# Tokens of a mixture of experts moved through DRAM rows instead of one-hot matmuls

## The chip, the cores and the metric

One core of a Trainium2 chip runs the whole program in one launch. The metric is device time in microseconds (us). Lower is better. Engines: PE (TensorE), DVE (VectorE), ACT (ScalarE), POOL (GpSimd) and SP (SyncE, which here only issues DMAs). DMAs issued by SP and by POOL stand in two different queues.

## The reference

Two layers over 256 tokens of width 1024, all in float32: a gated delta rule with a dense feed-forward, then windowed attention with a mixture of experts. Only the last part changes:

```python
def moe_swiglu(x, w_router, w_gate, w_up, w_down):          # x: 256 x 1024, 8 experts of width 3584
    logits = xf @ w_router
    top_val, top_idx = lax.top_k(logits, 2)
    gates = einsum('nk,nke->ne', softmax(top_val), one_hot(top_idx, 8))
    for e in range(8):
        h = jax.nn.silu(xf @ w_gate[e]) * (xf @ w_up[e])
        out = out + gates[:, e:e + 1] * (h @ w_down[e])
    return out
```

The sum `ALPHA * x + out` then goes through a layer norm, which is the output.

## The kernel before

Only the tokens routed to an expert are multiplied with its weights, up to 128 of them (a loop behind a branch, not taken here, handles more). The router (`logits`, `route`, `gates`) leaves three small tables with 8 columns per token: `sel` (is this expert chosen), `pos` (the token's place among that expert's tokens) and `gate`. `x[0]` and `x[1]` are the two blocks of 128 tokens, in SBUF.

**Expert loop.** `todo` runs over 8 experts `e` and 7 blocks `b` of 512 hidden columns, 56 blocks. In each, `gateup` multiplies the expert's gathered tokens `xg` with 512 columns of `w_gate` and of `w_up`; `hidden_moe` forms silu(gate) * up (`msg`: the activation at L1099, the product at L1101) and transposes it (L1105) into a high and a low part (`mhh`, `mhl`); `down` adds its product with 512 rows of `w_down` into two PSUM banks `acc[e]`. `down` of a block is issued after `gateup` of the next one.

**Weights.** Every weight arrives by `unit` in loads of 1 MiB, issued by SP (L127) into a ring of buffers `raw`, and is split into a rounded part `hi` (ACT, L136) and a remainder `lo` (DVE, L137), four pieces each. A product is three matmuls (`mm3`, L152 to L155). A block takes 6 loads, 24 pieces of `hi` and of `lo`, and 72 matmuls of 512 columns. `more_ring` widens the ring for the experts: after the first round it cycles over 10 buffers.

**Going to an expert.** `gather(e)`, issued after block 2 of the expert before: DVE builds two 128x128 one-hot matrices `Pe` (L1047), 16 float32 matmuls (L1053) multiply them with `x`, and the result is split into `xg` (L1067, L1068).

**Coming back.** `finish(e)`, issued after the last `down`: `Pe` is transposed (L1134) and copied (L1135), `acc` is split (`yh`, `yl`: L1140, L1141), 8 matmuls (L1144, L1145) spread the rows over the 256 tokens, and DVE adds them, scaled by `gate`, to `y` (L1147), four times 512 columns. `y` is set to `ALPHA * x` by POOL at expert 0, block 3 (L1167).

**Layer 0.** The change also adds DMAs there. The gated delta rule inverts triangular matrices. Diagonal blocks go to DRAM and back (`dA`, then `A`: L501, L506), DVE solves them in 15 steps (L517, L518), and the result goes through DRAM again (`dD`, then `DD`: L520, L522) to PE (L595). POOL masks `EdT` just before (L485).

**Order.** A scheduler places each engine's instructions; every engine runs its own list strictly in that order, so one that waits holds up all behind it.

Of the kernel before, what the change touches and what calls it, by code (L numbers as in the profile page):

```python
# [30 lines left out]
P = 128  # L31
# [17 lines left out]
C_ID, C_TRIU, C_TRIS, C_IOTA, C_J, C_MB, C_OH, C_W = 0, 128, 256, 384, 512, 640, 768, 896  # L49


def constants():
    import numpy as np
    c = np.zeros((P, C_W), np.float32)
# [17 lines left out]
def kernel(ctx: ExitStack, tc: tile.TileContext, A, out):  # L72
# [38 lines left out]
    def more_ring(c, name, bufs, before=(), after=(), keep=()):  # L111
        pool = c.enter_context(tc.tile_pool(name=name, bufs=bufs))
        more = [raw_in(pool, "raw")] * bufs
        raws[0] = chain(base, before, more, keep, after, cycle(base + more + list(keep)))
# [264 lines left out]
    nc.sync.dma_start(cst, A["consts"][:, P:])  # L379
# [59 lines left out]
    # projections, causal convolution and silu, channel-major  # L439
# [36 lines left out]
    # A' = strict lower of p_i k_i.k_j exp(gc_i - gc_j); inverse of I + A', first in diagonal blocks of 16  # L476
    Up = gp.tile([P, 2, 8, P], F32, name="Up")
    dA = dram.tile([16 * HS], F32, name="dA")
    for tb in range(2):
# [5 lines left out]
        G.affine_select(EdT[:, tb], EdT[:, tb], [[0, 8], [1, P]], OP.is_ge, 0.0, base=0, channel_multiplier=-1)  # L485
# [92 lines left out]
    # inverse of the diagonal blocks of 32, 64 and 128 from those of half the size  # L578
# [41 lines left out]

    before = None
# [11 lines left out]
    # chunk 0, state, chunk 1  # L633
# [332 lines left out]
    # router: the rank of each expert for a token, and its slot among the tokens of that expert  # L966
# [6 lines left out]
    sel, gate, pos = (rt.tile([P, 2, E], F32, name=n) for n in ("sel", "gate", "pos"))  # L973
# [12 lines left out]
    def route(tb, plg, done):  # L986
# [47 lines left out]

    with ExitStack() as mctx:
        more_ring(mctx, "ring_m", 4, [], [raw_in(per, "Bh"), raw_in(per, "lngb")],
                  [raw_in(per, t) for t in ("Al", "Bl", "Ah")])
        mp = mctx.enter_context(tc.tile_pool(name="moe", bufs=2))
        Pe = {}

        def gather(e):
            Pe[e] = mp.tile([P, 2, P], F32, name="Pe", tag="Pe")
# [7 lines left out]
            pg = [accb() if e == 0 else None for _ in range(2)]  # L1050

            def pick(k, tb):
                PE.matmul(pg[k // 4][:, (k % 4) * P:(k % 4 + 1) * P], x[tb][:, k * P:(k + 1) * P], Pe[e][:, tb, :],  # L1053
                          start=tb == 0 and (e > 0 or k % 4 == 0), stop=tb == 1 and (e > 0 or k % 4 == 3))

            if e == 0:
                for k in range(KC):
                    pick(k, 0)
            for g in range(2):
                if e:  # L1060
                    pg[g] = trb()
                for k in range(4 * g, 4 * g + 4):
                    if e:
                        pick(k, 0)
                    pick(k, 1)
                hi, lo = (t[:, 4 * g:4 * g + 4, :].rearrange("p a c -> p (a c)") for t in xg)
                S.copy(hi, pg[g])  # L1067
                V.tensor_sub(lo, pg[g], hi.bitcast(F32))  # L1068
            return xg, placed

        xg = {}
        xg[0], placed = gather(0)
# [4 lines left out]
        V.tensor_copy(cnti, cnt[0:1, :])  # L1077
        for tb in range(2):
            with tc.issue_after(placed.ins):
                gates(tb, lgs[tb])  # L1080
# [48 lines left out]

        def finish(e):  # L1130
# [140 lines left out]
```

## Time and profile before

| | |
|---|---|
| three runs | 1487.53, 1488.69, 1488.91 us; median 1488.69 |
| profiled execution, span from first to last instruction | 1484.7 us (the profile gives no other time of it) |
| median of the runs less that span | 4.0 us |
| PE, DVE, ACT, POOL busy | 97%, 85%, 68%, 2% of the span |
| DMA | 427.67 MB, 288 GB/s over the span |

A row of a timeline gives the start, the time from the first start to the last end of the merged instructions, engine, line, operation, tiles written and read, and their count. A row with windows gives a stretch, its length, the busy time of each engine with the count of instructions, TensorE's granted clock as a share of full speed, the DMA engines' share, and GB/s. In `--lines` style rows: count, total busy time and mean ns of one, then the idle time before and what ended it.

### The profile page before, as it was taken

To read this page: it belongs to the slowest core of one execution; us is meant where nothing else is said; L and a number is where in the kernel's file an instruction comes from. 1 tells how busy PE (TensorE), PEld (TensorE's weight loads), DVE (VectorE), ACT (ScalarE), POOL (GpSimd) and SP (SyncE) were. 2 spreads that over 40 slices of the span, in tenths; PEclk is the share of its full clock that TensorE was granted. 3 is DMA by queue.
4 is the path that set the end of the run, shared out by engine and by line. 5 is a ranking of instruction groups with operands and counts; after the bars stand their busy time and mean duration, and the time that the engine had idled before them with its cause. 6 is when DMAs were issued, how large, how long until landed. Compare 5 with 4: busy or idle time off the path is not lost. (4 is left out here: it accounts for less than half of the span.)

```text
span 1484.7 us, 20295 instructions
## 1 busy us (share of the span) xinstructions
PE 1447.1 (97%) x7023; PEld 1193.3 (80%) x7023; DVE 1256.1 (85%) x2296; ACT 1016.6 (68%) x1998; POOL 32.6 (2%) x56
## 2 busy tenths in 40 slices
PE   6999999999998999999999999999999999999995
PEld 5888788887877888888888878878888887887884
DVE  4875965555867999999998998999999999899997
ACT  4764454443534878878877777877887787777883
POOL 4000000001000200000000000000000000000000
PEclk9999999999998999999999999999999999999998
DMA  8631575553638899999999989999999999999980
GB/s 266 208 118 58 186 257 181 173 196 85 233 114 298 317 358 371 342 348 378 329 361 342 350 327 354 375 328 357 366 338 350 372 376 335 352 368 335 380 310 30
DMA packets 189308, 427.67 MB, mean 288 GB/s; under 512 B 12096, under 2 KB 19424, under 8 KB 189200
## 3 DMA queue, kind: packets, MB, share of 16 engines
q1 hardware_dynamic: 186512, 421.69, 79.0%
q0 software_dynamic: 1216, 3.98, 1.0%
q8 instruction: 57, 0.93, 0.3%
q10 hardware_dynamic: 1472, 0.66, 0.2%
q14 instruction: 51, 0.42, 0.1%
HBM read 422.99 MB, written 3.30 MB: 287 GB/s over the span
## 5 line engine op out<-in xcount | busy, mean ns | idle before, releaser
L137 DVE TENSOR_TENSOR lo<-raw,hi 128x512 fp32r<-128x512 f32 x1576 | 977.4, 684 | 104.3 <-ACT hi L136 95.6
L136 ACT CAST hi<-raw 128x512 fp32r<-128x512 f32 x1576 | 851.8, 619 | 167.4 <-PE acc L153 57.3
L152 PE MATMUL mm<-hi,xg 128*128 128x512 f32 x448 | 175.7, 392 | 0.2
L152 PE MATMUL acc<-hi,mhh 128*128 128x512 f32 x448 | 175.8, 402 | 0.0
L153 PE MATMUL acc<-hi,mhl 128*128 128x512 f32 x448 | 175.0, 391 | 0.0
L153 PE MATMUL mm<-hi,xg 128*128 128x512 f32 x448 | 175.0, 391 | 0.0
L152 PE MATMUL acc<-hi,xg 128*128 128x512 f32 x448 | 174.4, 389 | 0.0
L153 PE MATMUL acc<-hi,xg 128*128 128x512 f32 x448 | 174.3, 389 | 0.0
L155 PE MATMUL acc<-lo,mhh 128*128 128x512 f32 x448 | 148.1, 390 | 0.0
L155 PE MATMUL mm<-lo,xg 128*128 128x512 f32 x448 | 124.8, 391 | 0.5 <-DVE lo L137 0.3
L155 PE MATMUL acc<-lo,xg 128*128 128x512 f32 x448 | 121.9, 391 | 0.7
L155 PEld LDWEIGHTS acc<-lo,xg 128*128 128x128 f32 x448 | 84.1, 188 | 20.8 <-DVE lo L137 3.3
L155 PEld LDWEIGHTS mm<-lo,xg 128*128 128x128 f32 x448 | 84.1, 188 | 20.0 <-DVE lo L137 2.7
L152 PEld LDWEIGHTS mm<-hi,xg 128*128 128x128 f32 x448 | 84.1, 188 | 18.7 <-ACT hi L136 2.1
L155 PEld LDWEIGHTS acc<-lo,mhh 128*128 128x128 f32 x448 | 84.1, 188 | 18.5
L153 PEld LDWEIGHTS acc<-hi,xg 128*128 128x128 f32 x448 | 84.1, 188 | 17.4
L152 PEld LDWEIGHTS acc<-hi,xg 128*128 128x128 f32 x448 | 84.1, 188 | 17.3
L153 PEld LDWEIGHTS mm<-hi,xg 128*128 128x128 f32 x448 | 84.2, 188 | 17.2 <-DVE xg L1068 0.3
L153 PEld LDWEIGHTS acc<-hi,mhl 128*128 128x128 f32 x448 | 84.3, 188 | 15.9
L152 PEld LDWEIGHTS acc<-hi,mhh 128*128 128x128 f32 x448 | 84.2, 188 | 16.0
L1108 ACT CAST mhh<-tr 128x512 fp32r<-128x512 f32 x56 | 32.8, 585 | 90.5 <-PE tr L1105 90.5
L1099 ACT ACTIVATE msg<-mm 128x512 f32<-128x512 f32 x56 | 33.4, 596 | 46.5 <-PE mm L155 46.5
(359 smaller groups left out, 1717.9 us busy)
## 6 DMA issues: line engine op xcount, KB each, us to landing
raw<-in_moe_w_gate_dram SPq DMA_DIRECT2D x112, 1024.0 KB, 6.6
raw<-in_moe_w_up_dram SPq DMA_DIRECT2D x112, 1024.0 KB, 6.7
raw<-in_moe_w_down_dram SPq DMA_DIRECT2D x112, 1024.0 KB, 6.0
raw<-in_a_w_in_dram SPq DMA_DIRECT2D x12, 1024.0 KB, 5.4
raw<-in_ffn_w_gate_dram SPq DMA_DIRECT2D x11, 1024.0 KB, 5.2
raw<-in_ffn_w_up_dram SPq DMA_DIRECT2D x11, 1024.0 KB, 5.4
raw<-in_ffn_w_down_dram SPq DMA_DIRECT2D x11, 1024.0 KB, 4.9
raw<-in_b_w_in_dram SPq DMA_DIRECT2D x5, 1024.0 KB, 5.2
```

What stands on the lines that cost most here:

```text
L136: S.copy(hi[:, c], raw[:, c])
L137: subs.append(V.tensor_sub(lo[:, c], raw[:, c], hi[:, c].bitcast(F32)))
L152: PE.matmul(ps, xh(k), wh, start=first and k == 0, stop=False)
L153: PE.matmul(ps, xl(k), wh, start=False, stop=False)
L155: PE.matmul(ps, xh(k), wl, start=False, stop=last and k == n - 1)
L1099: S.activation(s, ps[0], AF.Silu)
L1108: S.copy(hh, p)
```

## The change

A token's rows now pass through DRAM for experts 1 to 7 on the way in and for experts 0 to 6 on the way out. Expert 0 still gathers with one-hot matmuls and expert 7 still comes back with them.

- **Layer 0**: ten POOL DMAs of 512 KB write zeros from a constant in DRAM to two DRAM tables, `xs` (seven) and `ys` (three), issued after the mask of `EdT` (`turn_z`). A table has 128 rows per expert and 256 spare rows.
- **Start of the experts**: `places` computes on POOL and DVE, for each token's first and second expert, the row in the tables (`keyi`) and the gate (`gat2`). Four indirect DMAs on POOL's queue scatter the rows of `x` to `xs`; two DMAs save `x` in `x3d`.
- **In**: `fetch(e)` loads 128 rows of `xs` (512 KB) at block 1 of the expert before; `gather(e)` at block 3 is 8 transposes on PE, and the split as before.
- **Out**: `keep(e)` copies `acc` with two ACT copies and stores 512 KB to `ys`. At expert 7 four indirect DMAs (`collect`) bring back each token's two rows, and DVE adds each with one 128x1024 operation (`yt * gat2 + y`). Expert 7's rows in `ys` are zero; `finish(7)` adds its part.
- **Ring**: 12 buffers instead of 10, until expert 6, block 4, where two go back to `y` and the layer norm's parameters; `y` is loaded there from `x3d` and scaled on POOL. The buffers of `x` serve as `xr` and `yt`.

```diff
+    with tc.issue_after(turn_z.ins):
+        for r in range(P, SPARE, P):
+            nc.gpsimd.dma_start(xs[r:r + P], zero)
+        for r in range(SPARE - P, ROWS, P):
+            nc.gpsimd.dma_start(ys_[r:r + P], zero)
...
+    def places():
+        sq = [P, 2, E]
+        row, spill, one, val = (rt.tile(sq, F32, name=n) for n in ("row", "spill", "one", "val"))
+        G.tensor_tensor(row, pos, cs(C_EX, E)[:, None, :].to_broadcast(sq), op=OP.add)
+        G.tensor_tensor(spill, cs(C_SP, 2)[:, :, None].to_broadcast(sq), row, op=OP.subtract)
+        G.tensor_scalar(val, pos, float(P), None, op0=OP.is_ge)
+        G.tensor_tensor(spill, spill, val, op=OP.mult)
+        G.tensor_tensor(row, row, spill, op=OP.add)
+        key = rt.tile([P, 2, 2], F32, name="key")
+        for j in range(2):
+            G.tensor_scalar(one, rank, float(j), None, op0=OP.is_equal)
+            for src, dst in ((row, key), (gate, gat2)):
+                G.tensor_tensor(val, one, src, op=OP.mult)
+                V.tensor_reduce(dst[:, j], val, axis=AX.X, op=OP.add)
+        V.tensor_copy(keyi, key)
...
+        def fetch(e):
+            xr[e] = per.tile([P, D], F32, name="xr", tag="x0")
+            nc.gpsimd.dma_start(xr[e], xs[e * P:(e + 1) * P])
...
-                    pg[g] = trb()
-                for k in range(4 * g, 4 * g + 4):
                     if e:
-                        pick(k, 0)
-                    pick(k, 1)
+                        PE.transpose(pc, xr[e][:, k * P:(k + 1) * P], ident)
...
+        for j in range(2):
+            for tb in range(2):
+                nc.gpsimd.indirect_dma_start(out=xs[:, :], out_offset=at(j, tb), in_=x[tb][:, :], in_offset=None)
         for tb in range(2):
+            nc.gpsimd.dma_start(x3d[tb * P:(tb + 1) * P], x[tb])
...
+        def keep(e):
+            yt = per.tile([P, D], F32, name="yt", tag="x1")
+            for h in range(2):
+                S.copy(yt[:, h * 512:(h + 1) * 512], acc[e][h])
+            nc.gpsimd.dma_start(ys_[e * P:(e + 1) * P], yt)
...
+        def collect(j, tb):
+            yt = per.tile([P, D], F32, name="yt", tag="x%d" % tb)
+            nc.gpsimd.indirect_dma_start(out=yt[:, :], out_offset=None, in_=ys_[:, :], in_offset=at(j, tb))
+            V.scalar_tensor_tensor(y[tb], yt, gat2[:, j, tb:tb + 1], y[tb], op0=OP.mult, op1=OP.add)
...
                 if prev[1] == NB - 1:
-                    finish(prev[0])
-            if b == 2 and e + 1 < NE:
-                xg[e + 1] = gather(e + 1)[0]
+                    keep(prev[0])
+            if b == 1 and e + 1 < NE:
+                fetch(e + 1)
+            if b == 3 and e + 1 < NE:
+                xg[e + 1] = gather(e + 1)
...
+            if e == NE - 1 and 1 <= b <= 4:
+                collect((b - 1) // 2, (b - 1) % 2)
```

**How the order moves.** First, DVE's list at the start of the experts, around the split of expert 0's `xg`, which PE's first products need (`mx`, `gate` and `gden` belong to the router's gates, `lo` to the weights). Before:

```order
L1011 TENSOR_REDUCE mx_4217<-lg_4148 128x1
L1011 TENSOR_REDUCE mx_4226<-lg_4162 128x1
L137 TENSOR_TENSOR lo<-raw,hi 128x512
L1013 TENSOR_SCALAR gate<-lg_4148,mx_4217 128x8
L1013 TENSOR_SCALAR gate<-lg_4162,mx_4226 128x8
L137 TENSOR_TENSOR lo<-raw,hi 128x512
L1015 TENSOR_TENSOR gate<-gate,sel 128x8 x2
L137 TENSOR_TENSOR lo<-raw,hi 128x512
L1068 TENSOR_TENSOR xg<-acc,xg 128x512
L1076 TENSOR_REDUCE cnt<-tr 128x1
L1068 TENSOR_TENSOR xg<-acc,xg 128x512
```

And now, the same stretch and the rows that follow it:

```order
L148 TENSOR_TENSOR lo<-raw,hi 128x512
L1033 TENSOR_SCALAR gate<-lg_4161,mx_4231 128x8
L1033 TENSOR_SCALAR gate<-lg_4174,mx_4240 128x8
L1073 TENSOR_REDUCE key<-val 128x2
L148 TENSOR_TENSOR lo<-raw,hi 128x512
L1035 TENSOR_TENSOR gate<-gate,sel 128x8 x2
L148 TENSOR_TENSOR lo<-raw,hi 128x512
L1114 TENSOR_TENSOR xg<-acc,xg 128x512
```

```order
L148 TENSOR_TENSOR lo<-raw,hi 128x512
L1073 TENSOR_REDUCE gat_4191<-val 128x2
L148 TENSOR_TENSOR lo<-raw,hi 128x512
L1073 TENSOR_REDUCE key<-val 128x2
L148 TENSOR_TENSOR lo<-raw,hi 128x512
L1073 TENSOR_REDUCE gat_4191<-val 128x2
L1074 CAST keyi<-key 128x4
```

A reduction of `key` that waits for POOL stands ahead of the split of `xg`, and three more with a cast among the next pieces of `lo`; between two of them POOL has to multiply again, since `val` is one buffer.

Second, POOL's list from the mask of `EdT` in layer 0 to the start of layer 1. Before, and now:

```order
L485 AFFINE_SELECT EdT<-EdT 128x1024 x2
L739 DMA relb<-in_rel_bias_dram 32x16
L743 MEMSET rr 16x384
L746 DMA rd<-rr 16x384
L785 DMA rw<-in_moe_router_dram 128x8x8
```

```order
L496 AFFINE_SELECT EdT<-EdT 128x1024 x2
L638 DMA xs<-in_consts_dram 128x1024 x7
L640 DMA ys<-in_consts_dram 128x1024 x3
L760 DMA relb<-in_rel_bias_dram 32x16
L764 MEMSET rr 16x384
L767 DMA rd<-rr 16x384
L806 DMA rw<-in_moe_router_dram 128x8x8
```

The ten fills of zeros come right behind the mask, on a queue that had nothing to do for a while.

Third, DVE's list where expert 6 ends and expert 7 begins (`mhl` of expert 7's block 0 is the first row but one of each). Before, and now:

```order
L137 TENSOR_TENSOR lo<-raw,hi 128x512 x4
L1109 TENSOR_TENSOR mhl<-tr,mhh 128x512
L1141 TENSOR_TENSOR yl<-acc,yh 128x512
L137 TENSOR_TENSOR lo<-raw,hi 128x512 x3
L1147 SCALAR_TENSOR_TENSOR y<-tr,gate,y 128x512 x2
L1141 TENSOR_TENSOR yl<-acc,yh 128x512
L137 TENSOR_TENSOR lo<-raw,hi 128x512
L1147 SCALAR_TENSOR_TENSOR y<-tr,gate,y 128x512 x2
L137 TENSOR_TENSOR lo<-raw,hi 128x512 x16
L1101 TENSOR_TENSOR msg<-msg,acc 128x512
```

```order
L148 TENSOR_TENSOR lo<-raw,hi 128x512 x4
L1162 TENSOR_TENSOR mhl<-tr,mhh 128x512
L148 TENSOR_TENSOR lo<-raw,hi 128x512 x12
L1211 SCALAR_TENSOR_TENSOR y<-yt,gat_4191,y 128x1024
L148 TENSOR_TENSOR lo<-raw,hi 128x512 x4
L1211 SCALAR_TENSOR_TENSOR y<-yt,gat_4191,y 128x1024
L148 TENSOR_TENSOR lo<-raw,hi 128x512 x4
L1154 TENSOR_TENSOR msg<-msg,acc 128x512
L148 TENSOR_TENSOR lo<-raw,hi 128x512 x4
L1162 TENSOR_TENSOR mhl<-tr,mhh 128x512
L148 TENSOR_TENSOR lo<-raw,hi 128x512 x4
L1211 SCALAR_TENSOR_TENSOR y<-yt,gat_4191,y 128x1024
L148 TENSOR_TENSOR lo<-raw,hi 128x512 x8
L1211 SCALAR_TENSOR_TENSOR y<-yt,gat_4191,y 128x1024
```

The splits and sums of `finish(6)` are gone. In their place four sums of 128x1024 that wait for the indirect loads stand among the pieces of `lo`; 12 pieces separate `mhl` from the first. All other rows of these engines in the experts stand as before but for the missing `Pe`, `yl` and `y` rows and `xg`, which comes one block later.

## Rows read from the trace of the kernel before

**Rows 1.** The first rows of the page, and busy us of the engines, their share of the span and their instructions.

```profile
span 1484.7 us, 20295 instructions
...
PE 1447.1 (97%) x7023; PEld 1193.3 (80%) x7023; DVE 1256.1 (85%) x2296; ACT 1016.6 (68%) x1998; POOL 32.6 (2%) x56
```

**Rows 2.** Timeline of ACT, the activation of `msg` (L1099), one in each of the 56 blocks: expert 0 block 1, expert 1 blocks 4 and 5, expert 7 blocks 0 and 2, and the last.

```profile
493.39 0.59 ACT L1099 ACTIVATE msg<-mm 128x512 f32<-128x512 f32 x1
...
670.85 0.59 ACT L1099 ACTIVATE msg<-mm 128x512 f32<-128x512 f32 x1
...
687.64 0.59 ACT L1099 ACTIVATE msg<-mm 128x512 f32<-128x512 f32 x1
...
1344.75 0.60 ACT L1099 ACTIVATE msg<-mm 128x512 f32<-128x512 f32 x1 [1.36 <-PE mm L155]
...
1381.79 0.60 ACT L1099 ACTIVATE msg<-mm 128x512 f32<-128x512 f32 x1 [1.37 <-PE mm L155]
...
1449.00 0.60 ACT L1099 ACTIVATE msg<-mm 128x512 f32<-128x512 f32 x1 [1.38 <-PE mm L155]
```

**Rows 3.** Timeline of PE: the gather of expert 1 and the row after it; the first and the eighth product of a weight buffer in expert 1, block 6 (the first of `w_up`); the transposes of `msg` in the last block and the row after them.

```profile
521.22 3.73 PE L1053 MATMUL tr<-Pe,x 128*128 128x128 f32 x32
524.71 0.48 PE L152 MATMUL mm<-hi,xg 128*128 128x512 f32 x1
...
704.12 0.39 PE L152 MATMUL acc<-hi,xg 128*128 128x512 f32 x1
...
705.70 0.39 PE L153 MATMUL acc<-hi,xg 128*128 128x512 f32 x1
...
1456.96 0.60 PE L1105 MATMUL tr<-ident,msg 128*128 128x128 f32 x4
1457.32 0.48 PE L152 MATMUL acc<-hi,mhh 128*128 128x512 f32 x1
```

**Rows 4.** Timeline of DVE in the same block.

```profile
704.37 2.51 DVE L137 TENSOR_TENSOR lo<-raw,hi 128x512 fp32r<-128x512 f32 x4 [0.22 <-issue]
```

**Rows 5.** Who waited for whom in SP's queue: us in total, times, longest us; the timeline of SP, the first and the last of the 14 loads of expert weights issued before 470 us (the first row holds two); and four windows.

```profile
SPq L127 <- DVE lo L137: 1081.4, 370, 28.0
...
405.05 4.14 SPq L127 DMA_DIRECT2D raw<-in_moe_w_gate_dram  x2
...
469.99 0.50 SPq L127 DMA_DIRECT2D raw<-in_moe_w_up_dram  x1
...
445.00:450.00 5.00, 5.00 (x34) 4.46 (x34) 3.19 (x10) 3.54 (x10) 0.00 (x0) 1.00 1.05 399
560.00:600.00 40.00, 40.00 (x182) 33.12 (x181) 38.29 (x63) 33.88 (x64) 0.00 (x0) 1.00 1.02 374
1240.00:1340.00 100.00, 100.00 (x470) 83.37 (x469) 93.29 (x156) 79.56 (x152) 0.00 (x0) 1.00 1.00 363
1440.00:1445.00 5.00, 5.00 (x26) 4.12 (x25) 4.83 (x9) 4.21 (x9) 0.00 (x0) 1.00 0.38 145
```

**Rows 6.** Groups of instructions by line, shapes apart: the sums of `finish`, and a DVE operation on 128x1024 of layer 0.

```profile
L1147 DVE SCALAR_TENSOR_TENSOR y<-tr,gate,y 128x512 f32<-128x512 f32 x32 | 22.5, 745 | 2.0 <-PE tr L1145 1.7
...
L563 DVE TENSOR_TENSOR EdT<-acc,EdT 128x1024 f32<-128x1024 f32 x2 | 2.4, 1218 | 0.2 <-PE acc L560 0.2
```

**Rows 7.** DMA issues: destination and source, queue, count, KB each, median us from issue to landing.

```profile
raw<-in_moe_w_gate_dram SPq DMA_DIRECT2D x112, 1024.0 KB, 6.6
raw<-in_moe_w_up_dram SPq DMA_DIRECT2D x112, 1024.0 KB, 6.7
raw<-in_moe_w_down_dram SPq DMA_DIRECT2D x112, 1024.0 KB, 6.0
...
lngb<-in_ln_g_dram SPq DMA_DIRECT2D x4, 512.0 KB, 5.8
...
dD<-DD POOLq DMA_DIRECT2D x2, 512.0 KB, 8.3
dA<-Ed SPq DMA_DIRECT2D x2, 512.0 KB, 2.9
```

**Rows 8.** Timeline of DVE at the start of the experts, and of POOL in layer 0, operations on 128x16: the first pair spaced widely, the second closely.

```profile
472.25 0.17 DVE L1006 COPY pos<-mm 128x8 f32<-128x8 f32 x1 [1.38 <-PE mm L1005]
...
473.45 0.36 DVE L1013 TENSOR_SCALAR gate<-lg,mx 128x8 f32<-128x8 f32 x2
...
20.11 0.61 POOL L391 TENSOR_SCALAR m<-t 128x16 f32<-128x16 f32 x1
20.80 0.55 POOL L392 TENSOR_SCALAR y<-m 128x16 f32<-128x16 f32 x1
...
26.13 0.22 POOL L403 TENSOR_TENSOR w<-w,s 128x16 f32<-128x16 f32 x1
26.44 0.25 POOL L404 TENSOR_SCALAR w<-w 128x16 f32<-128x16 f32 x1
```

**Rows 9.** Layer 0: timeline of POOL (the second mask of `EdT`) and of DVE (first step of the solution), and a window.

```profile
50.77 1.09 POOL L485 TENSOR_SCALAR_AFFINE_SELECT EdT<-EdT 128x1024 f32<-128x1024 f32 x1 [1.52 <-ACT EdT L484]
...
69.73 0.17 DVE L517 TENSOR_TENSOR tm<-A,D 128x15 f32<-128x15 f32 x1
...
65.00:70.00 5.00, 5.00 (x24) 3.87 (x22) 5.00 (x16) 3.49 (x9) 0.00 (x0) 1.00 0.79 227
```

**Rows 10.** Timeline of DVE, the last split of a weight.

```profile
1462.43 2.50 DVE L137 TENSOR_TENSOR lo<-raw,hi 128x512 fp32r<-128x512 f32 x4 [1.12 <-ACT hi L136]
```

More of the change, by code (lines that the diff above doesn't have):

```diff
@@ L109, with more_ring, go @@
     raws = [cycle(base)]
-    def more_ring(c, name, bufs, before=(), after=(), keep=()):
+    def more_ring(c, name, bufs, keep=()):
         pool = c.enter_context(tc.tile_pool(name=name, bufs=bufs))
-        more = [raw_in(pool, "raw")] * bufs
-        raws[0] = chain(base, before, more, keep, after, cycle(base + more + list(keep)))
+        turns = base + [raw_in(pool, "raw")] * bufs + list(keep)
+        def go():
+            while True:
+                turns.append(turns.pop(0))
+                yield turns[-1]
+        raws[0] = go()
+        return turns
     quanta = [4]
@@ L972 @@
     G.affine_select(before, before, [[1, E], [-1, E]], OP.is_gt, 0.0, base=0, channel_multiplier=0)
-    sel, gate, pos = (rt.tile([P, 2, E], F32, name=n) for n in ("sel", "gate", "pos"))
+    sel, gate, pos, rank = (rt.tile([P, 2, E], F32, name=n) for n in ("sel", "gate", "pos", "rank"))
     def logits(tb):
@@ L1033, with at, onehot @@
     cnti = rt.tile([1, 1], I32, name="cnti")
+    keyi = rt.tile([P, 2, 2], I32, name="keyi")
+    gat2 = rt.tile([P, 2, 2], F32, name="gat2")
+    x3d = dram.tile([T, D], F32, name="x3d")
+    def places():
[13 more added lines that the diff above has]
+        V.tensor_copy(keyi, key)
+    def at(j, tb):
+        return bass.IndirectOffsetOnAxis(ap=keyi[:, j, tb:tb + 1], axis=0)
     with ExitStack() as mctx:
-        more_ring(mctx, "ring_m", 4, [], [raw_in(per, "Bh"), raw_in(per, "lngb")],
-                  [raw_in(per, t) for t in ("Al", "Bl", "Ah")])
+        ylng = [raw_in(per, t) for t in ("Bh", "lngb")]
+        turns = more_ring(mctx, "ring_m", 4, [raw_in(per, t) for t in ("Al", "Bl", "Ah")] + ylng)
         mp = mctx.enter_context(tc.tile_pool(name="moe", bufs=2))
         Pe = {}
-        def gather(e):
-            Pe[e] = mp.tile([P, 2, P], F32, name="Pe", tag="Pe")
+        xr = {}
+        def onehot(e):
+            Pe[e] = mp.tile([P, 2, P], F32, name="Pe", tag="Pe", bufs=1)
             with ExitStack() as late:
@@ L1077 @@
         V.tensor_copy(cnti, cnt[0:1, :])
+        with tc.issue_after(placed.ins):
+            for tb in range(2):
+                gates(tb, lgs[tb])
+            places()
+        for j in range(2):
+            for tb in range(2):
+                nc.gpsimd.indirect_dma_start(out=xs[:, :], out_offset=at(j, tb), in_=x[tb][:, :], in_offset=None)
         for tb in range(2):
-            with tc.issue_after(placed.ins):
-                gates(tb, lgs[tb])
+            nc.gpsimd.dma_start(x3d[tb * P:(tb + 1) * P], x[tb])
         NB = EF // 512
@@ L1184 @@
                                 op0=OP.is_equal, op1=OP.mult)
+            xo = [op_.tile([P, D], F32, name="xo%d" % tb) for tb in range(2)]
+            for tb in range(2):
+                nc.sync.dma_start(xo[tb], x3d[tb * P:(tb + 1) * P])
             xg2 = op_.tile([P, KC, P], F32, name="xg2")
```

60 lines of the change are left out of this document (36 added, 24 removed).

## The prediction

> **What bounds the kernel now.** I read the page first: PE is busy for 97% of the span, DVE 85%, ACT 68%, and 20295 instructions take 1484.7 us [rows 1]. A share is an average over stages, so next comes the step of the expert loop: the activations of `msg`, one per block. Two neighbouring plain blocks are 687.64 − 670.85 = 16.79 us apart [rows 2]. PE explains that alone: eight products of one weight buffer start 705.70 − 704.12 = 1.58 us apart, 0.226 each; 72 of them are 16.3, and the four transposes of `msg` 1457.32 − 1456.96 = 0.36 [rows 3]. DVE needs less: its splits run at (2.51 − 0.68) / 3 = 0.61 apiece, if the first row's latency at one end (0.68) is left out [rows 4]; 24 splits and two more operations of that size make 15.9, so it gains 0.9 us per block on PE. The loads are ahead as well: SP waits 370 times for the split that frees a buffer, 1081.4 us in all [rows 5]. So **PE sets the pace**, and a PE instruction taken away there is time gained.
>
> **How much is not plain blocks.** From expert 0's block 1 to the last block are 54 steps, 1449.00 − 493.39 = 955.61 us [rows 2]. At 16.79 they would take 906.7; 48.9 us are over. Nothing else stands there but seven gathers and seven `finish`. A gather takes PE 524.71 − 521.22 = 3.49 [rows 3], seven 24.4. What is left, 24.5, is 3.5 for a `finish`. A check: from 1344.75 to 1381.79, across one `finish`, are 37.04 us, two plain steps and 3.46 [rows 2].
>
> **The change part by part.**
> - *In, gathers 1 to 7.* 16 float32 matmuls go, 8 transposes come. At 0.09 each [rows 3] they take 0.72, say 0.8 with the change of banks: 5.6 in all, and 24.4 − 5.6 = **18.8 less**. The split into `xg` is as before. The two `Pe` (L1047) leave DVE, which had slack: nothing.
> - *Out, experts 0 to 6.* The seven `finish` leave PE: **24.5 less**. DVE loses 28 of 32 sums of 0.745 [rows 6]; it was not the bound. The two ACT copies of `keep` at 0.59, by the activation of that shape [rows 2], find room, since ACT is busy for 33.88 of 40 us in a stretch of plain blocks [rows 5]: nothing. They also free `acc`, which PE next writes in the block after.
> - *Rows in DRAM, in time?* After the scatters, `fetch(1)` has to land before the gather behind block 3, at about 493.39 + 3 × 16.79 = 543.8. A POOL transfer of 512 KB took 8.3 us [rows 7]. If `keyi` is there by 480, four scatters one after another end at 513, the fetch at 522: some 20 us of cover. It is gone if each takes over 12.8. Later fetches have two blocks, 33 us. Nothing.
> - *Start.* A reduction of `key` stands on DVE ahead of the split of expert 0's `xg`, on which PE waits. It needs six POOL operations after `pos`, which is there at 472.4; DVE would reach it at 473.45 + 0.36 = 473.8 [rows 8]. POOL's small operations follow each other in 0.31 (26.13 to 26.44) to 0.69 us (20.11 to 20.80) [rows 8], so six end at 474.3 to 476.5: a wait of 0.5 to 2.7. Three later reductions each wait for two more POOL operations (0.6 to 1.4), with a split of 0.61 to do meanwhile: 0 to 0.8 each. Ends 0.5 and 5, and I take **2 more**, by the closer spacing, since these operations are of 128x16.
>  The Trainium skill ("SBUF — State Buffer", section "Who interferes with whom") speaks against this place: a DVE instruction with two SBUF inputs, as the split of a weight is, blocks a GpSimd instruction that reads SBUF until it is over. Each of the six would then sit out one split, and the sum would be about 2 us higher; no row of this trace has the two side by side.
> - *Layer 0.* The ten fills come from 50.77 + 1.09 = 51.9 on [rows 9], 512 KB each. At 374 to 399 GB/s [rows 5] that is 13 to 14 us, if reading and writing in DRAM cost no more than a load. They end near 66, ahead of DVE's first solving step (69.73), whose input `A` goes through DRAM just then; from 65 to 70 DVE is busy all of the time and the DMA engines 0.79 [rows 9]. If `A` was not late the cost is nothing; if the fills push most of their 14 us in front of it, about 10. I take **3 more**.
> - *Collects.* `keep(6)` finds `acc` ready where a block starts (T0); block 6 of expert 1 stands in for it, where T0 = 704.12 − 24 × 0.226 = 698.7 [rows 3]. Its place in DVE's list puts the first sum at about the split at 704.37 [rows 4], 5.7 after T0. The row takes longer to come: ACT 0.7, the store as `dA` 2.9, the load as `lngb` 5.8 [rows 7], together 9.4; with POOL's 8.3 for both, 17.3; with 2.9 for both, 6.5. So DVE stands still for 3.7 (0.8 to 11.6), and the splits behind it are what PE needs next. The four sums take 4 × 1.22 [rows 6] = 4.9. Against this stand DVE's lead, about 1.8 (the split at 704.37 ends at 706.88 [rows 4]; PE needs it after eight products of `hi`, twice over, near 708.6), and its gain over a block and a half, 1.4. 3.7 + 4.9 − 3.2 = **5.4 more** (2.5 to 13.3).
> - *Ring, `y` late, x3d*: 12 buffers for 10 help loads that already wait for buffers; POOL scales `y` within expert 6, with a block of time. Nothing.
>
> **Sum.** −18.8 − 24.5 + 2 + 3 + 5.4 = −32.9: a span of 1451.8. The median of the runs stands 4.0 above the profiled span (1488.7 to 1484.7), and I add that: **1456 us**. All low ends give 1448, all high ends 1474.
>
> **Rivals.**
> 1. **The loads become the bound.** Faster blocks ask for more per us, and 13 MiB of rows join. 336 weight loads [rows 7] less the 14 issued by 470 [rows 5] are 337.6 MB; with 13.6 MB of rows, 351.3 MB remain from 480 on. After the last landing stay one split of four pieces (3.1) and what follows the last split today, 1484.7 − (1462.43 + 2.50) = 19.8 [rows 10]. The time is then 480 + 351.3 MB / rate + 22.9 + 4.0. For 1456 the rate must be 370 GB/s. Over 1240 to 1340 the DMA engines moved 363 at a share of 1.00; if that is all they can do, the time is **1474.5**, still faster. Against it: 374 over 40 us and 399 over 5 [rows 5], SP's long waits for buffers, and that by 1440 to 1445, with the last blocks still to come, the rate is down to 145 [rows 5], the loads being nearly through.
> 2. **The same mechanism, slower than before.** If scattered rows and DRAM-to-DRAM traffic between the weights hold the mean below 358 GB/s, the sum passes 1488.7; at 350 it is **1510.6**. For it: a share of 1.00 at 363. Against it: the same engines reached 374, and only 4% of the bytes are new.
>  The Trainium skill ("SBUF — State Buffer", section "Summary: rules for kernel authors") says to reckon with about 358 GB/s between HBM and SBUF. With that the formula of rival 1 gives 1488, no change at all; the windows of 374 and 399 are above it, so I give this outcome little.
> 3. **Late rows.** POOL's DMAs go on taking 8.3 us in a row: the collects cost 13.3 rather than 5.4, and the fills in layer 0 cost 10 rather than 3. With the one the time is 1464, with the other 1463, with both **1471**. For it: both POOL transfers of 512 KB in the trace took 8.3 against 2.9 on SP's queue.
> 4. **Nothing gained on PE**, because DVE sets the pace as soon as PE is relieved: about 1488. Against it: per expert DVE has 7 × 15.9 + 1.3 = 112.6 us, PE still 7 × 16.79 + 0.8 = 118.3.
>
> **How the numbers follow.** Forecast 0.60, rival 1 0.18, rival 3 0.14, rivals 2 and 4 0.05 and 0.03. A measurement here can tell about 0.2%, 3 us, from no change. Forecast, rival 1 and rival 3 all end below 1485: faster 0.92. Rival 4 gives same 0.03, rival 2 slower 0.05. The range goes from the low ends of all costs (1448, and 1 off for what is rounded), 1447, to just above rivals 1 and 3, 1476.
>
> **What would show it.** After the change, plain blocks still 16.8 apart and PE over 97% busy; steps with a gather 0.8 longer than plain ones and those of experts 0 to 6 with `keep` no longer at all; `collect` sums with an idle time of 1 to 12 us before the first, and `msg` in expert 7 late by as much; the split of `xg` at the start some 2 us later; the solving steps of layer 0 later by 0 to 10. Rival 1 would show as PE and the splits waiting for loads, and SP hardly waiting for buffers; rival 3 as long landings of POOL's DMAs. The forecast is wrong if PE has over 60 us of idle time in the experts, or if the blocks grow beyond 17 us.

## The result: 1503.3 us, slower by 1%, and the profile after

| | before | after |
|---|---|---|
| median | 1488.3 us | 1503.3 us |
| runs | 1487.5 to 1488.9 | 1501.9 to 1506.6 |
| ratio | | 1.010 (1.0084 to 1.0115) |
| span of the profiled execution | 1484.7 us | 1504.9 us |

1456 was forecast. The profiled executions are not the medians: the one of after is the run of 1506.6 us, the slowest of its four, so spans after minus before give +20.2 us where the medians give +15.0. The page after, beside [rows 1]: 468 instructions are gone, PE is busy about as long as before.

```profile
span 1504.9 us, 19827 instructions
...
PE 1446.3 (96%) x6785; PEld 1168.8 (78%) x6785; DVE 1233.2 (82%) x2251; ACT 1013.0 (67%) x1991; POOL 63.7 (4%) x103
```

238 PE instructions fewer in the same busy time: those that are left must have become longer. The activations of `msg` (now L1152) tell where. ACT's timeline: expert 0 block 1; expert 1 blocks 2, 3, 4; expert 3 blocks 0 and 1; expert 7 blocks 1 and 2; the last.

```profile
511.76 0.59 ACT L1152 ACTIVATE msg<-mm 128x512 f32<-128x512 f32 x1
...
651.04 0.59 ACT L1152 ACTIVATE msg<-mm 128x512 f32<-128x512 f32 x1
...
668.34 0.59 ACT L1152 ACTIVATE msg<-mm 128x512 f32<-128x512 f32 x1
...
686.53 0.59 ACT L1152 ACTIVATE msg<-mm 128x512 f32<-128x512 f32 x1
...
860.42 0.60 ACT L1152 ACTIVATE msg<-mm 128x512 f32<-128x512 f32 x1 [1.60 <-PE mm L166]
...
878.86 0.60 ACT L1152 ACTIVATE msg<-mm 128x512 f32<-128x512 f32 x1 [0.40 <-PE mm L166]
...
1371.99 0.60 ACT L1152 ACTIVATE msg<-mm 128x512 f32<-128x512 f32 x1 [0.41 <-PE mm L166]
...
1399.62 0.60 ACT L1152 ACTIVATE msg<-mm 128x512 f32<-128x512 f32 x1 [1.38 <-PE mm L166]
...
1469.12 0.60 ACT L1152 ACTIVATE msg<-mm 128x512 f32<-128x512 f32 x1 [1.60 <-PE mm L166]
```

Beside [rows 2]: a plain step is 668.34 − 651.04 = **17.30 us**, where it was 16.79. The step with a gather (to 686.53) is 0.89 longer than that, the step into expert 3's block 1 is 18.44, and one step, into block 2 of expert 7, is 27.63. From the first row to the last are 957.4 us, where they were 955.6. PE's timeline in that stretch, first and eighth product of the first buffer of `w_up`, as in [rows 3]:

```profile
703.53 0.40 PE L163 MATMUL acc<-hi,xg 128*128 128x512 f32 x1
...
705.17 0.40 PE L164 MATMUL acc<-hi,xg 128*128 128x512 f32 x1
```

(705.17 − 703.53) / 7 = 0.234 us from product to product, where [rows 3] have 0.226. No wait stands between them and the granted clock is 1.00 in both. 72 × 0.0075 = 0.54 explains the longer block.

Layer 0: the landing of `dA` (7th column: median us) took 2.9 in [rows 7]; after:

```profile
dA<-Ed SPq DMA_DIRECT2D x2, 512.0 KB, 15.4
```

POOL's timeline has the fills behind the mask, DVE's the first solving step at 82.61, 69.73 in [rows 9], after 12.89 us of waiting for that data:

```profile
50.61 1.09 POOL L496 TENSOR_SCALAR_AFFINE_SELECT EdT<-EdT 128x1024 f32<-128x1024 f32 x1 [1.51 <-ACT EdT L495]
51.65 3.72 POOL L638 DMA_DIRECT2D xs<-in_consts_dram  x7
```

```profile
82.61 0.18 DVE L528 TENSOR_TENSOR tm<-A,D 128x15 f32<-128x15 f32 x1 [12.89 <-DMA A<-dA]
```

PE runs dry there, which it did not before: it stands for 10.97 us. When it goes on, its granted clock is 0.50, the lower of its two levels, up to 91.3 us, and that costs 2.8 us more. PE's timeline, and a window with the busy us of PE, PEld, DVE, ACT and POOL:

```profile
85.72 0.87 PE L553 MATMUL tr<-ident,vT 128*128 128x128 f32 x3 [10.97 <-DVE D L529]
```

```profile
86.00:91.00 5.00, 5.00 (x20) 4.14 (x18) 4.34 (x14) 2.60 (x8) 0.00 (x0) 0.50 0.65 213
```

Expert 7, DVE: the first sum of `collect` (L1211) waits 8.88 us for the indirect load, the pieces of `lo` behind it come late by as much. PE stands for 7.32 us, up to 1383.96, and then works at a granted clock of 0.50 up to 1388.4.

```profile
1366.42 6.71 DVE L148 TENSOR_TENSOR lo<-raw,hi 128x512 fp32r<-128x512 f32 x11 [0.32 <-ACT hi L147]
1382.01 1.28 DVE L1211 SCALAR_TENSOR_TENSOR y<-yt,gat,y 128x1024 f32<-128x1024 f32 x1 [8.88 <-DMA yt<-ys,keyi]
1383.22 2.49 DVE L148 TENSOR_TENSOR lo<-raw,hi 128x512 fp32r<-128x512 f32 x4
```

Expert 3, ACT: the first copy of `keep` (L1186) waits 1.28 us for the last product of `down`, and the next piece of `hi` stands behind it. Experts 4 to 7 look alike. In experts 1 and 2 the scheduler put two pieces of `hi` ahead of the copy (third row, expert 2): it does not wait, and these steps are plain.

```profile
871.15 0.59 ACT L1186 COPY yt<-acc 128x512 f32<-128x512 f32 x1 [1.28 <-PE acc L166]
871.63 0.62 ACT L147 CAST hi<-raw 128x512 fp32r<-128x512 f32 x1
...
748.73 0.59 ACT L1186 COPY yt<-acc 128x512 f32<-128x512 f32 x1
```

Put together, as spans after minus before (the stage of the experts starts with its first product of `xg`). Gathers and `finish` are taken from the steps that hold them, less plain steps of 16.80 and 17.30, their means:

| part | forecast | measured |
|---|---|---|
| seven gathers | −18.8 | −18.5 (0.88 to 0.98 above a plain step, 6.6 in all, where they were 25.1) |
| seven `finish` | −24.5 | −23.2 (2.0 to 5.2 each above plain steps before, none now) |
| plain blocks | 0 | +27.0 (54 × 0.50) |
| fills in layer 0 | +3 | +13.8 (first product of `hTh` at 316.7, was 302.9; +11.4 to +13.1 in the profiles of e1, e4, e6 and e7, with the same fills) |
| `collect` | +5.4 | +10.3 |
| `keep` | 0 | +5.8 (five steps of 18.45 instead of 17.30) |
| layer 1 and start of the experts | +2 | +4.3 (first product of `xg` at 494.1, was 476.0, less the 13.8) |
| rest | | +0.7 |
| sum | −32.9 | +20.2 |

### The profile page after: what moved, and what is told of

Read it like the earlier page. It is cut to its first block, busy times and chain, and to the rows that moved or that the text cites. A ratio compares the mean times of both kernels' runs of the same rounds, so it can differ in the third digit from the quotient of the medians.

```text
span 1504.9 us, 19827 instructions
## 1 busy us (share of the span) xinstructions
PE 1446.3 (96%) x6785; PEld 1168.8 (78%) x6785; DVE 1233.2 (82%) x2251; ACT 1013.0 (67%) x1991; POOL 63.7 (4%) x103
## 5 line engine op out<-in xcount | busy, mean ns | idle before, releaser
L163 PE MATMUL mm<-hi,xg 128*128 128x512 f32 x448 | 180.4, 403 | 2.7 <-ACT hi L147 2.7
L164 PE MATMUL acc<-hi,mhl 128*128 128x512 f32 x448 | 178.2, 398 | 0.0
L164 PE MATMUL acc<-hi,xg 128*128 128x512 f32 x448 | 177.7, 397 | 0.0
L163 PE MATMUL acc<-hi,xg 128*128 128x512 f32 x448 | 177.6, 396 | 0.0
L164 PE MATMUL mm<-hi,xg 128*128 128x512 f32 x448 | 177.6, 396 | 0.0
L166 PE MATMUL acc<-lo,mhh 128*128 128x512 f32 x448 | 154.7, 396 | 0.0
L166 PE MATMUL acc<-lo,xg 128*128 128x512 f32 x448 | 125.1, 400 | 7.5 <-DVE lo L148 7.3
L1152 ACT ACTIVATE msg<-mm 128x512 f32<-128x512 f32 x56 | 33.4, 597 | 56.7 <-PE mm L166 56.7
```

What stands on the lines that cost most here:

```text
L163: PE.matmul(ps, xh(k), wh, start=first and k == 0, stop=False)
L164: PE.matmul(ps, xl(k), wh, start=False, stop=False)
L166: PE.matmul(ps, xh(k), wl, start=False, stop=last and k == n - 1)
L1152: S.activation(s, ps[0], AF.Silu)
```

## Experiments

### Why is every product of the experts longer?

The program's allocation shows one thing that the diff does not say: new small tables and a wider constants' tile moved all that lies behind them in SBUF. `xg`, `mhh` and `mhl`, the stationary operands, started at the same offset modulo 256 bytes as `hi` and `lo`, the moving ones (both 128); now it is 32 against 192. Theory A holds that to be the cause, theory B the larger ring and the added traffic, theory C a PE that is busy more densely.

**e1**: two paddings in the changed kernel.

```diff
-    cst = per.tile([P, C_W - P], F32, name="cst")
+    cst = per.tile([P, 832], F32, name="cst")
...
         key = rt.tile([P, 2, 2], F32, name="key")
+        rt.tile([P, 40], F32, name="pad")
```

> The changed kernel with two paddings in SBUF and nothing else: the constants' tile is 3328 bytes wide (it was 3072 before the change and 3112 after it) and an unused tile of 160 bytes follows the tables of the router. With that xg, mhh and mhl start at the same offset modulo 256 bytes as the split weights hi and lo (128 and 128), as they did before the change; in the changed kernel it is 32 against 192. Theory A (place in SBUF): products of 512 columns start 0.227 us apart again instead of 0.234, a plain block takes 16.8 instead of 17.3, and 54 blocks give back 54 x 0.51 = 27 us: 1476 us. Theory B (the larger ring and the added rows disturb PE's reads): nothing changes, 1503. Theory C (PE is busy more densely and therefore slower): nothing changes, 1503.

1479.0 us, ratio to before 0.9931 (0.9914 to 0.9947). ACT's timeline, two activations of `msg` of plain blocks of expert 4:

```profile
1003.15 0.60 ACT L1153 ACTIVATE msg<-mm 128x512 f32<-128x512 f32 x1 [1.37 <-PE mm L166]
...
1019.95 0.60 ACT L1153 ACTIVATE msg<-mm 128x512 f32<-128x512 f32 x1 [1.35 <-PE mm L166]
```

16.80 us a step: the unused bytes gave 24 us back, and the change is 0.7% faster than the kernel before. The other 3 of the 27 went to the steps that are not plain: the one into block 2 of expert 7 is 11.4 above a plain step (10.3 without the bytes), those with `keep` 1.25 (1.15), those with a gather 0.9 to 1.1.

**e2**: the kernel before with 32 unused bytes.

```diff
     cnti = rt.tile([1, 1], I32, name="cnti")
+    rt.tile([P, 8], F32, name="pad")
```

> The kernel before with one unused tile of 32 bytes after the tables of the router, which moves the experts' ring, xg, mhh and mhl by 32 bytes against hi and lo; no instruction changes. Theory A: products 0.234 us apart in the experts alone, plain blocks of about 17.3, 54 x 0.5 = 27 us more: 1515 us, while layer 0 keeps 0.227. Theories B and C: no change, 1488.

1512.6 us, ratio 1.0158 (1.0141 to 1.0175). The same timeline, expert 1 blocks 5 and 6:

```profile
695.17 0.59 ACT L1100 ACTIVATE msg<-mm 128x512 f32<-128x512 f32 x1
...
712.40 0.59 ACT L1100 ACTIVATE msg<-mm 128x512 f32<-128x512 f32 x1
```

17.23 a step, with as many buffers, the same traffic and the same instructions as in the kernel before: B and C fall.

**e9** puts the same 32 bytes behind the ring (`mp.tile([P, 8], F32, name="pad", bufs=1)` as the first tile of the pool `moe`), **e10** and **e11** put 64 and 128 bytes where e2 has 32, **e12** 192 bytes ahead of `hTh` in layer 0:

```diff
+        fp.tile([P, 48], F32, name="pad", bufs=1)
         hT = tuple(fp.tile([P, NF, T], F32R, name=n, bufs=1) for n in ("hTh", "hTl"))
```

> The kernel before with the unused 32 bytes not ahead of the experts' ring but behind it, at the start of the pool of xg, msg, mhh and mhl: the buffers of the loads stay where they were, the stationary operands move by 32 bytes. Theory A': what counts is the place of the stationary operand against hi and lo: 0.233 us between products in the experts and 1512 us, as with the tile ahead of the ring. Rival: the ring's place counts (loads into buffers that start 32 bytes off): 0.227 and 1488.

> The kernel before with 64 unused bytes ahead of the experts' ring. xg then starts at a multiple of 64 bytes, as in the kernel before, but 64 bytes off hi and lo modulo 256. Theory A (the distance to hi and lo counts): slow, 0.233 us, like hTh and hTl in layer 0 of the kernel before, which are also 64 off. Rival (a start that is no multiple of 64 is slow in itself): 0.227.

> The kernel before with 128 unused bytes ahead of the experts' ring, xg 128 bytes off hi and lo modulo 256. If the distance counts modulo 256: 0.233 us and about 1512. If it counts modulo 128 or less: 0.227 and 1488.

> The kernel before with 192 unused bytes ahead of hTh and hTl, the hidden values of layer 0's feed-forward, which then start at the same place modulo 256 as hi and lo. Theory A: the 260 products of that stage, 0.233 us apart in both kernels (from 303 to 364 us), come 0.227 apart, and the stage is 260 x 0.0067 = 1.7 us shorter. Rival (something else of that stage makes them slow): no change there.

Each had one run: 1509.8, 1512.1, 1508.6 and 1486.0 us, beside 1487.9 for the kernel before. The mean from product to product, over all pairs without a wait between them, and the distance of the stationary operand's start from that of `hi`, modulo 256 bytes:

| kernel, operand | distance | us | pairs |
|---|---|---|---|
| before, `xg` | 0 | 0.2269 | 2647 |
| before, `hTh`, `hTl` | 64 | 0.2333 | 261 |
| after, `x1Th` (it and `hi` at 192) | 0 | 0.2273 | 463 |
| after, `xg` | 96 | 0.2343 | 2641 |
| e1, `xg` | 0 | 0.2269 | 2639 |
| e2, e9, `xg` | 32 | 0.2333 | 2647 |
| e10, `xg` (at 192, `hi` at 128) | 64 | 0.2333 | 2648 |
| e11, `xg` | 128 | 0.2326 | 2647 |
| e12, `hTh`, `hTl` | 0 | 0.2267 | 261 |

PE's timeline of layer 0's down product in the kernel before, and in e12 (first and fourth of four products):

```profile
317.29 0.40 PE L152 MATMUL acc<-hi,hTh 128*128 128x512 f32 x1
...
317.99 0.39 PE L153 MATMUL acc<-hi,hTl 128*128 128x512 f32 x1
```

```profile
317.25 0.39 PE L152 MATMUL acc<-hi,hTh 128*128 128x512 f32 x1
...
317.93 0.39 PE L153 MATMUL acc<-hi,hTl 128*128 128x512 f32 x1
```

0.233 and 0.227. e9 leaves the ring where it was and is slow, so the loads' buffers are not it. e10 starts at a multiple of 64 and is slow, while `x1Th` of the changed kernel, at the same 192, is fast because `hi` is at 192 too: the distance counts, not the start. Only distance 0 was fast among 0, 32, 64, 96 and 128. In e12 the 260 products of `hTh` and `hTl` take 60.0 us from first to last, 61.7 in the kernel before, the 1.7 that were expected. Nor are the other engines the cause: in 61 of these pairs no instruction of ACT, DVE or POOL ran beside the products, and they are 0.2337 apart in the kernel before, 0.2267 in e12. Distance 0 is not all of it: the pairs of `mhh` and `mhl` in the kernel before, also at 0, average 0.2284, some of them at 0.231 to 0.236. Why the chip does this the runs do not tell.

### Are the fills the 14 us of layer 0?

**e3**: the same ten DMAs behind the load of the bias table, at 367 us.

```diff
-    with tc.issue_after(turn_z.ins):
...
+        turn_z = nc.gpsimd.dma_start(bT, ...)
+        with tc.issue_after(turn_z.ins):
+            for r in range(P, SPARE, P):
+                nc.gpsimd.dma_start(xs[r:r + P], zero)
```

> The changed kernel with the ten fills of zeros issued on POOL's queue behind the load of the bias table bT at the start of layer 1's attention (about 380 us) and not behind the mask of EdT in layer 0 (52 us). Theory: the store of dA lands about 3 us after its issue and not 15, DVE's solving steps start some 13 us earlier, and the whole moves by as much: 1490 us. Rival: the fills delay the weights of the attention instead, and 5 to 10 of the 13 us come back there: 1495 to 1500. Second rival: layer 0 is late for another reason: 1503.

1503.5 us: nothing gained. The 14 us of layer 0 were back (first product of `hTh` at 302.3), and 12.1 us came again where the fills now stood (from there to the last product of `x2Th` 118.0 us, 105.8 in the kernel before). The window (us of PE, PEld, DVE, ACT, POOL; granted clock, DMA share, GB/s):

```profile
375.00:402.00 27.00, 16.21 (x83) 13.40 (x81) 11.81 (x21) 5.68 (x14) 1.55 (x3) 0.81 1.01 386
```

The DMA engines are full, and two weight loads issued into the fills land after 18.9 and 21.5 us, 5.7 and 5.8 in the kernel before. PE works 16 of 27 us: it stands for 10.79 us, and over the window its granted clock is 0.81. The first rival was right, and more than it said.

**e5**: the fills wait for `DD`, the last of the round trip.

```diff
+    z1 = gp.tile([P, 1], F32, name="z1")
+    turn_z = G.tensor_copy(z1, DD[:, 1, 0, 0:1])
     with tc.issue_after(turn_z.ins):
```

> The changed kernel with the ten fills behind a one-column copy on POOL that reads DD, so that they start when DVE's solution has come back from DRAM (about 98 us) and not behind the mask (52 us). Theory (the price is that the fills share the DMA engines with the round trip of dA, and there is a stretch with few loads right behind it): dA lands after 3 us, the first product of layer 1's norm output and all that follows stands some 12 us earlier than in the changed kernel, and little comes back: 1490 to 1493 us. Rival (5 MiB cost their 13 us wherever they are put, as at 380 us): 1501 to 1504.

1491.9 us, 11.4 less than the changed kernel. `dA` lands early again; and the windows from 95 to 115 us of the kernel before and of e5:

```profile
dA<-Ed SPq DMA_DIRECT2D x2, 512.0 KB, 3.2
```

```profile
95.00:115.00 20.00, 20.00 (x164) 19.13 (x163) 14.59 (x41) 10.55 (x22) 0.00 (x0) 1.00 0.16 41
```

```profile
95.00:115.00 20.00, 20.00 (x167) 19.23 (x166) 14.22 (x39) 9.89 (x21) 5.38 (x11) 1.00 0.88 265
```

The DMA engines had stood at 0.16 there; PE is as busy with the fills as without. The price of the 5 MiB was their place. What they take of the DMA engines is not small: from the first issue to the last landing 22.4 us (98.22 to 120.58), though the next weight load is issued only at 114.1.

### The collects

**e4**: one block later in the program.

```diff
-            if e == NE - 1 and 1 <= b <= 4:
-                collect((b - 1) // 2, (b - 1) % 2)
+            if e == NE - 1 and 2 <= b <= 5:
+                collect((b - 2) // 2, (b - 2) % 2)
```

> The changed kernel with the four collects one block later (expert 7, blocks 2 to 5, not 1 to 4): their DMAs can go as early as before, DVE's sums stand some 17 us later. Theory (DVE stands still for the indirect load and the splits behind it reach PE late): the wait of 8.9 us before the first sum is gone, and the long step of 27.6 us falls to 18 to 19: 1494 us. Rival (the sums' own 4.9 us of DVE are what PE misses): 5 us or more of the 10 stay: 1499.

1504.0 us, no difference; but the edit did not do what it says. The scheduler left the sums where they were in DVE's list, 12 pieces of `lo` behind `mhl`, and the first waited 8.95 us. It answers nothing. **e6** holds each sum in the order:

```diff
+            with tc.issue_after(subs[-1].ins):
-            V.scalar_tensor_tensor(y[tb], yt, gat2[:, j, tb:tb + 1], y[tb], op0=OP.mult, op1=OP.add)
+                V.scalar_tensor_tensor(y[tb], yt, gat2[:, j, tb:tb + 1], y[tb], op0=OP.mult, op1=OP.add)
```

> The changed kernel with the collects in blocks 2 to 5 of expert 7 and, unlike the kernel with blocks 2 to 5 alone, whose sums the scheduler left where they were in DVE's list, with each sum held in the order behind the last split of its block: the four sums stand one per block. Theory: no wait before the first sum (8.9 us), DVE makes up one sum of 1.2 us per block; the step of 27.6 us falls to about 17.3 and one or two of the next are up to 1 us longer: 1493 us. Rival (the load would have been in time, the splits are late because of the sums): 5 us or more stay: 1499.

1494.3 us. ACT's timeline, `msg` in blocks 1 and 2 of expert 7:

```profile
1370.89 0.60 ACT L1152 ACTIVATE msg<-mm 128x512 f32<-128x512 f32 x1 [0.40 <-PE mm L166]
...
1388.19 0.60 ACT L1152 ACTIVATE msg<-mm 128x512 f32<-128x512 f32 x1 [1.60 <-PE mm L166]
```

The step of 27.63 is 17.30. Without the wait, and with one sum per block, the sums cost nothing but 0.4 us in the last step. The edit takes away the wait and spreads the sums at once; what the sums would cost close together but without a wait, no run shows.

### The copies of keep

**e7**: DVE instead of ACT, called behind the splits of the next block.

```diff
-                S.copy(yt[:, h * 512:(h + 1) * 512], acc[e][h])
+                    V.tensor_copy(yt[:, h * 512:(h + 1) * 512], acc[e][h])
...
+                if then is not None and w is wu_:
+                    keep(then)
...
-                if prev[1] == NB - 1:
-                    keep(prev[0])
```

> The changed kernel with the two copies of keep on DVE instead of ACT and placed behind the splits of the next block. Theory: the steps into block 1 of experts 3 to 7 (18.45 us) are longer than plain ones because the first copy stands in ACT's list ahead of the next hi and waits 1.28 us for the last product of down; without it they are 17.3, 5 x 1.15 = 6 us less: 1497 us. Rival (PE waits there for the banks of acc, whoever copies): still 18.4 or more, 1503 or later.

1498.5 us, 4.8 less; from the first activation of `msg` to the last 962.2 us, 5.4 less. The step into block 1 of expert 3 on ACT's timeline is 17.29:

```profile
857.59 0.60 ACT L1154 ACTIVATE msg<-mm 128x512 f32<-128x512 f32 x1 [1.60 <-PE mm L166]
...
874.88 0.60 ACT L1154 ACTIVATE msg<-mm 128x512 f32<-128x512 f32 x1 [1.58 <-PE mm L166]
```

All five such steps are plain now. Half a microsecond of the expected six went elsewhere: the later store makes the step into block 2 of expert 7 28.16 rather than 27.63. The edit changes both engine and place; that the place counts is what experts 1 and 2 of the changed kernel show, where ACT copies behind two pieces of `hi` and nothing is lost.

### All four together

**e8**: e1, e5, e6 and e7 in one kernel.

> The changed kernel with all four: place in SBUF as before the change, fills behind DD, the sums of collect one per block, the copies of keep on DVE. If the four causes are separate their gains add up: 24.5 + 12 + 10 + 6 = 52 us less than 1503: 1451 us. If two of them share a wait, or if the faster blocks run into the loads (6 MiB per 16.8 us), 1460 or more.

**1450.9 us**, ratio to before 0.9734 (0.9711 to 0.9756): 37 us faster than the kernel before, 52 faster than the change as it was made. That it is 1451 to a tenth is luck: the four runs go from 1445.0 to 1454.6, and one by one the edits gave 24.3, 11.4, 9.1 and 4.8, 49.7 in all. ACT's timeline, `msg` of expert 4 blocks 0 and 1, expert 7 blocks 2 and 3; DVE's, the first sum; POOL's, the issue of its load; and a window:

```profile
955.11 0.60 ACT L1157 ACTIVATE msg<-mm 128x512 f32<-128x512 f32 x1 [1.38 <-PE mm L166]
...
971.90 0.60 ACT L1157 ACTIVATE msg<-mm 128x512 f32<-128x512 f32 x1 [1.36 <-PE mm L166]
...
1345.27 0.60 ACT L1157 ACTIVATE msg<-mm 128x512 f32<-128x512 f32 x1 [0.91 <-PE mm L166]
...
1366.37 0.60 ACT L1157 ACTIVATE msg<-mm 128x512 f32<-128x512 f32 x1 [5.67 <-PE mm L166]
```

```profile
1358.42 1.28 DVE L1218 SCALAR_TENSOR_TENSOR y<-yt,gat,y 128x1024 f32<-128x1024 f32 x1 [3.24 <-DMA yt<-ys,keyi]
```

```profile
1341.12 11.14 POOL L1216 DMA_INDIRECT yt<-ys,keyi  x1 [6.92 <-DMA ys<-yt]
```

```profile
900.00:1000.00 100.00, 100.00 (x453) 82.55 (x452) 95.97 (x159) 82.26 (x158) 0.54 (x1) 1.00 1.01 378
```

Blocks are 16.79 apart at 378 GB/s, so the loads are not the bound. What is left is a step of 21.10 in expert 7: the first sum still waits 3.24 us. `keep(6)` stores later, but the load that follows would be in time if it took what it takes in the changed kernel, 7.9 us. Here POOL is 11.14 us at its issue (1.03 there), and it lands after 17.2. Why, no run shows.

## Why the prediction was wrong, point by point

**The step that failed** is one the sum did not contain: that a block which the diff leaves alone still takes 16.79 us. It was written as an expectation (plain blocks "still 16.8 apart", and the forecast wrong "if the blocks grow beyond 17 us"), and just that came: 17.30. The cause is the place of the tiles in SBUF (e1, e2, e9 to e12), and its 27 us outweigh either gain, more than half of what the forecast missed. With the old place alone the change would have been faster, 1479.0, though still outside the range. A clue stood in the trace of before: products of `hTh` 0.233 us apart, those of `xg` 0.227, same shape, same clock. It was not looked for.

**The gains** were right: 41.7 measured, 43.3 forecast. The gathers cost 0.95 above a plain step instead of 0.8; `finish` went entirely. That each `finish` cost 3.5 was a mean: they ran from 2.0 to 5.2, which the one step looked at, 3.46, could not tell.

**The fills** were mis-sized: 13.8 against 3 with an upper end of 10. The 14 us of transfer held only if reading and writing in DRAM cost no more than a load, and they did cost more: 22.7 us from the first issue to the last landing (51.65 to 74.32, and not near 66), 22.4 in e5. And `dA`, issued behind them on another queue (59.44 and 61.50), landed only after all ten had, at 75.15 and 76.65: 15.4 us against 2.9. What the sum had no term for is the clock: a pause of PE was priced by its length, and 2.8 of the 13.8 are the stretch at 0.50 behind it.

**The collects** stayed within their bounds (2.5 to 13.3): a wait of 8.88 and not 3.7. The store took 7.0 us (1366.16 to 1373.13), the indirect load 7.9 (1374.00 to 1381.92), near the 8.3 of POOL's transfers in [rows 7] and not the 2.9 and 5.8 of SP's that were taken. Part of the 10.3 is again PE's clock, at 0.50 for 4.4 us behind the pause. The Trainium skill ("DMA: Bandwidth & Descriptors", section "Anatomy of one DMA — SWDGE (gpsimd) path") gives about 2.0 us and the bytes at 436 GB/s, an estimate of 3.2 us for 512 KB; beside the weights it took more than twice that, and the measurement decides.

**keep** was put at nothing since ACT has room. It has, but the copy stands in ACT's list ahead of `hi` and waits for PE: 1.15 us, in five of the seven experts. Room on an engine is not enough where its list is kept in order.

**The start** cost 2.8 of the 4.3 us. That it is near the 2 forecast is luck, since it is not the wait that was priced. The other 1.5 are in the attention, where PE waits 1.74 us for a load (to 399.39); the kernel before does not, but in e2 it does (1.86), so the change need not be the cause. POOL, DVE and PE at the start, and a window:

```profile
488.17 0.72 POOL L1066 TENSOR_TENSOR spill<-spill,val 128x16 f32<-128x16 f32 x1
...
489.26 0.22 POOL L1072 TENSOR_TENSOR val<-one,row 128x16 f32<-128x16 f32 x1
```

```profile
487.68 0.34 DVE L1092 TENSOR_SCALAR Pe<-cst,pos,sel 128x128 f32<-128x128 f32 x1
...
488.13 0.67 DVE L148 TENSOR_TENSOR lo<-raw,hi 128x512 fp32r<-128x512 f32 x1
...
489.51 0.17 DVE L1073 TENSOR_REDUCE key<-val 128x2 f32<-128x16 f32 x1 [0.44 <-POOL val L1072]
```

```profile
488.07 6.24 PE L1111 MATMUL acc<-Pe,x 128*128 128x128 f32 x28 [0.51 <-DVE cnti L1124]
494.06 0.48 PE L163 MATMUL mm<-hi,xg 128*128 128x512 f32 x1
```

```profile
488.00:494.00 6.00, 5.93 (x28) 5.93 (x29) 4.15 (x18) 0.93 (x3) 1.25 (x4) 0.50 1.03 392
```

The reduction of `key` waits 0.44. The time is in expert 0's gather: from the second `Pe` to the first product are 494.06 − 487.68 = 6.38 us, where they were 3.55 in the kernel before (472.45 to 476.00). Two things differ. The change also reorders these products: before, those of the first 128 tokens, which need only the first `Pe`, came ahead of all others, and 8 of the 32 PE rows had started when the second `Pe` did; now it is 4, and 28 are left. Four rows more are 0.9 us. And the rows are 0.213 us apart while the granted clock is 0.50, 0.112 at 1.00: in the kernel before the clock rose at 473.76, with 18 rows to go, here only at 494.1, behind the last. That is 1.8. The place in SBUF has no part in it: e1 and e8 have the same places, and the 28 rows take 4.81 us in e1, where the clock rose at 490.5, and 6.17 in e8, where it rose at 480.1, behind them:

```profile
487.48 4.81 PE L1112 MATMUL acc<-Pe,x 128*128 128x128 f32 x28 [0.51 <-DVE cnti L1125]
```

```profile
474.20 6.17 PE L1114 MATMUL acc<-Pe,x 128*128 128x128 f32 x28 [0.51 <-DVE cnti L1127]
```

The stretch at 0.50 has other ends in other executions of the same instructions (463.9 to 474.1 in e9, 460.2 to 473.8 in e12, both the kernel before with unused bytes), so the 1.8 is a difference of two executions, and how much of it is the change no run shows.

By the rule of the Trainium skill ("SBUF — State Buffer", section "Who interferes with whom") that a DVE instruction with two SBUF inputs blocks a GpSimd instruction reading SBUF, each of POOL's operations would have sat out a split. The trace agrees for the one that met a split: 0.72 us at 488.17, beside the split from 488.13 to 488.80, where its neighbours took 0.22. The others met none. The prediction says that no row of the trace before has the two side by side, and there it misread its own [rows 8]: splits ran from 19.93 to 21.21, over the operations that took 0.61 and 0.55, and none at 26.13 to 26.69, where they took 0.22 and 0.25.

**The rivals.** The loads did not become the bound: SP still waited 1036 us for the splits to free buffers, in 355 waits, and e8 ran at 378 GB/s. That is more than the 358 by which the Trainium skill ("SBUF — State Buffer", section "Summary: rules for kernel authors") reckons; the measurement decides. DVE did not become the bound either (rival 4): e8's blocks are 16.79. Late rows (rival 3) came in full, 10.3 + 13.8 against 13.3 + 10. The rival for a slower kernel had the right sign by a wrong mechanism, and 0.05 was far too little for it.

## What to carry to other kernels

A tile added anywhere moves what lies behind it, and here the distance modulo 256 bytes between the stationary and the moving operand of a product was worth 3% of PE's time. Compare the spacing of products of one shape within a trace, before a change and after it, and pad a new tile so that the distance stays. Ten bulk transfers on one queue held up a small round trip that started behind them on another: issue such transfers in a stretch where the DMA engines stand idle. What waits in an engine's ordered list is priced by what stands behind it, not by the engine's busy share. And a pause of PE can cost more than its length, so look at the granted clock behind it.

## What the runs showed of the hardware that was not expected

- 512-column products with a 128x128 stationary operand came 0.227 us apart at distance 0 (0.228 for `mhh` and `mhl`) and 0.233 to 0.234 at 32, 64, 96 and 128 bytes, at a granted clock of 1.00 in both.
- Ten DRAM-to-DRAM DMAs of 512 KB on POOL's queue took 22.7 us from first issue to last landing (22.4 in e5) and made a 512 KB store on SP's queue land after 15.4 us instead of 2.9, behind all ten.
- After pauses of 10.97 us (the changed kernel, layer 0) and 7.32 us (its expert 7) PE went on at a granted clock of 0.50, for 5.6 and 4.4 us. With PE paused 10.79 of 27 us in e3, its granted clock over that window was 0.81, that is, part of the window at the lower of its two levels.
- POOL was 11.14 us at the issue of one indirect load in e8, 1.03 us at the same issue in the changed kernel.
